# Retention in a two-layer diffusion trunk: tables first, rotation and zeta products on GpSimd, chunk states and chunk products as steps of the attention from the fifth pair of tiles on

## The chip, the cores and the metric

One core of a Trainium2 chip runs the whole program. The metric is the device time of one execution, in microseconds. The engines are TensorE (PE in the profile), VectorE (DVE), ScalarE (ACT), GpSimd (POOL) and SyncE (SP); each runs its own list of instructions strictly in order, and the lists meet through semaphores. DMA transfers are issued from the queues of SP (SPq) and ACT (ACTq).

## What is computed

The reference runs two layers on 128 context tokens and 1024 latent tokens (nine tiles of 128 rows; tile 8 is the context). In each layer one projection feeds four groups of heads (retention, Fourier mixing, latent attention, Hyena convolution), whose outputs go side by side through one output projection, and then a gated feed-forward layer follows. The change concerns the retention, which is run forward and backward over chunks of 128 rows:

```python
xi = jnp.exp((i[:, None] + 1.0) * log_gamma[None, :])
zeta = jnp.exp((C - 1.0 - i)[:, None] * log_gamma[None, :])
g_chunk = jnp.exp(C * log_gamma)
kv = jnp.einsum('bnchd,bnche->nbhde', kc * zeta[None, None, :, :, None], vc)

def step(S, kv_j):
    return g_chunk[None, :, None, None] * S + kv_j, S

s_final, s_prev = lax.scan(step, s0, kv)
cross = jnp.einsum('bnchd,nbhde->bnche', qc * xi[None, None, :, :, None], s_prev)
return (inner + cross).reshape(B, L, H, dv), s_final
```

Before that q and k of the latent rows are rotated (`axial_rope`); after it each head's output is normalised over its 64 channels and multiplied by a gate, `silu(rg) * o`.

## The kernel before, in words

A layer has three parts. `phase1` computes the projection and prepares the Hyena and latent-attention operands; `phase2` runs Fourier mixing, retention and attention; `phase3` multiplies the joined outputs by the output projection (tile name `wo`), and after it comes the feed-forward part.

**`phase2`.** The kernel is written in one order and a scheduler places each instruction on its engine's list, by the blocks' priorities (`tc.high_priority(offset=...)`) and by when its operands should be there; on the chip the lists are fixed. The Fourier part has offset 600. The retention's preparation has offset 100 and consists of three functions:

- `ret_rope` loads q and k of all tiles (`rqk`, 128x512 per tile) and rotates the eight latent tiles. The helper `rope` issues four products per tile, two of 128x256 into a scratch tile (`rtmp`) and two of 128x512 on `rqk`. They run on DVE.
- `ret_tables` makes the decay tables from eight numbers: `rzt` (zeta), `rgt` (chunk decay), `rxi` and the masks `rD` (some 25 DVE instructions on 128x8 and smaller, then four pairs of L1050 and L1051 on larger tiles). Its scratch lies in `Sall[:, 4:6]`.
- `ret_states` clears `Sall` (two memsets on POOL), then for each of the nine tiles forms k times zeta (`rkz`, two 128x256 products on DVE), multiplies it with v on PE (`pskv`, four groups), copies the blocks into `Sall` on ACT, and at the end runs the chain over the chunks in both directions on DVE (L161, 28 instructions).

**`attention`.** It runs over 20 pairs of tiles (four heads, per head four pairs of latent tiles and the context tile). At n it issues the scores of pair n (`sc` on PE, the scaled running minimum `pr` L930 on DVE, the exponential L933 on ACT), the transposes of pair n-1 (`pstr`, split into `ph`/`pl` or `pth`/`ptl` on ACT and DVE) and the product with v of pair n-2 (`po`); then it calls `beside(n)`, first at n = 2. In the kernel before `beside` takes one step of the retention's groups: `ret_group` handles three tiles (`ret_tile`, one step each), then a step of statistics (`rmu`, `rsq`, `rvr`, an inverse square root in eleven small DVE instructions) and a step of gating, in which `ro` (128x768) is multiplied on POOL and DVE, transposed on PE (`psr<-konst,ro`, L1173), copied to `rot` on ACT and stored to `mixR` from ACTq. Three groups of five steps fill n = 2 to 16.

**`phase3`.** SP loads the eight row blocks of the output projection (`woraw`, 512 KB each), which ACT and DVE split (`woh`, `wol`), and for each tile the four stored parts (`mix<-mixR`, `mixF`, `mixA`, `mixH`), split into `mixs`. Its memory is the memory that `phase2` gives back, so a load there waits until the last reader of what lay in its place is done.

Of the kernel before, what the change touches and what calls it, by code (L numbers as in the profile page):

```python
# [10 lines left out]
F32 = mybir.dt.float32  # L11
# [3 lines left out]
ALU = mybir.AluOpType  # L15
# [4 lines left out]
P = 128  # L20
# [3 lines left out]
CTX = 8  # L24
# [75 lines left out]
class Kern:  # L100
# [950 lines left out]
            V.tensor_tensor(out=Dm[:, h], in0=tm[:, 0], in1=tm[:, 1], op=ALU.add)  # L1051
        return zt, gt, Dm, xi

    def ret_rope(self, l, keep):

        nc = self.nc
        tabs = keep.tile([P, 2, 8, 64], F32, name="ropeR")
        nc.sync.dma_start(tabs, self.A["ropeR"])
        self.qk = keep.tile([P, NT, 512], F32, name="rqk")
        part = [keep.tile([P, 8, 64], F32, name="rtmp", tag=tg) for tg in ("rD", "rxi")]  # L1060
        for t in range(NT):
            if t % 3 == 0:
                nc.sync.dma_start(self.qk[:, t:t + 3], self.proj[l][:, t:t + 3, 256:768])
            if t < CTX:
                self.rope("v", self.qk[:, t].rearrange("p (h d) -> p h d", h=8), tabs[:, :, t], part[t % 2], 8, 64)
        return keep.tile([P, 8, 2, 2, P], F32, name="Sall")

    def ret_states(self, l, zt, gt, Sall, keep, pool, psp):


        nc, A = self.nc, self.A
        kvc = pool.tile([P, 4, P], F32, name="kvc", tag="rqkT")[:, 0:2].rearrange("p a (b e) -> p a b e", b=2)
        kzs = keep.tile([P, 2, 2, 4, 64], F32, name="rkz", tag="ropeR")
        for hh in range(2):
            nc.gpsimd.memset(Sall[64 * hh:64 * hh + 64, :, :, :, 64 - 64 * hh:P - 64 * hh], 0.0)
        for d in range(2):
            for hh in range(2):
                q = slice(64 * hh, 64 * hh + 64)
                nc.sync.dma_start(Sall[q, 7 * d, :, d, q], A["sret"][l, q, :, d])
        for t in range(NT):  # L1080
            if t % 3 == 0:
                v3 = pool.tile([P, 3, 512], F32, name="rv", tag="rvg")[:, :, 0:256]
                nc.sync.dma_start(v3, self.proj[l][:, t:t + 3, 768:1024])
            v = v3[:, t % 3]
            qk = self.qk[:, t].rearrange("p (h d) -> p h d", h=8)
            kz = kzs[:, t % 2]
            for d in range(2):
                self.tt("v", kz[:, d], qk[:, 4:8], zt[:, d].unsqueeze(2).broadcast_to([P, 4, 64]), ALU.mult)
            ps = psp.tile([P, 2, 2, P], F32, name="pskv", tag="r")
            for pr in range(2):  # L1090
                for d in range(2):
                    nc.tensor.matmul(ps[:, pr, d], kz[:, d, 2 * pr:2 * pr + 2].rearrange("p h d -> p (h d)"),
                                     v[:, P * pr:P * pr + P], start=True, stop=True)
            for hh in range(2):
                q = slice(64 * hh, 64 * hh + 64)
                if t == CTX:
                    nc.scalar.activation(kvc[q], ps[q, :, :, q], AF.Copy)
                    continue
                for d, dst in ((0, t + 1), (1, t - 1)):
                    if 0 <= dst < 8:  # L1100
                        nc.scalar.activation(Sall[q, dst, :, d, q], ps[q, :, d, q], AF.Copy)

        nc.sync.dma_start(A["o_st"][l], kvc)
        for d, order in ((0, range(1, 8)), (1, range(6, -1, -1))):
            for t in order:
                prev = t - 1 if d == 0 else t + 1
                for k in range(2):
                    self.stt(Sall[:, t, k, d], Sall[:, prev, k, d], gt[:, k, d:d + 1], Sall[:, t, k, d], ALU.mult, ALU.add)

    def ret_tile(self, l, t, vg, o, Dm, xi, Sall, pool, psp):  # L1110

        nc = self.nc
        lat = t < CTX
        nc.sync.dma_start(vg, self.proj[l][:, t, 768:1280])
        ps = psp.tile([P, 4, P], F32, name="psr", tag="r")
        for j in range(4):
            nc.tensor.transpose(ps[:, j], self.qk[:, t, j * P:j * P + P], self.ident)
        qkT = pool.tile([P, 4, P], F32, name="rqkT", tag="rqkT")
        nc.scalar.activation(qkT, ps, AF.Copy)
        if lat:  # L1120
            qx = pool.tile([P, 2, 2, P], F32, name="rqx")
            self.tt("g", qx, qkT[:, 0:2].unsqueeze(2).broadcast_to([P, 2, 2, P]), xi, ALU.mult)

        sT = pool.tile([P, 4, P], F32, name="rsT")
        pe = [psp.tile([P, 2, P], F32, name="psr", tag="r") for _ in range(2)]
        for e in range(2):
            q = slice(64 * e, 64 * e + 64)
            for pr in range(2):
                nc.tensor.matmul(pe[e][:, pr], qkT[q, 2 + pr], qkT[q, pr], start=True, stop=True)
            nc.vector.tensor_tensor(out=sT[:, e::2], in0=pe[e], in1=Dm[:, e::2], op=ALU.mult)  # L1130

        pi = psp.tile([P, 4, 64], F32, name="psr", tag="r")
        for pr in range(2):
            both = pi[:, 2 * pr:2 * pr + 2].rearrange("p h e -> p (h e)")
            if lat:
                nc.tensor.matmul(both, qx[:, pr, 0], Sall[:, t, pr, 0], start=True, stop=False)
            for h in (2 * pr, 2 * pr + 1):
                nc.tensor.matmul(pi[:, h], sT[:, h], vg[:, 64 * h:64 * h + 64], start=not lat, stop=not lat)
            if lat:
                nc.tensor.matmul(both, qx[:, pr, 1], Sall[:, t, pr, 1], start=False, stop=True)  # L1140
        nc.scalar.activation(o, pi, AF.Copy)
# [94 lines left out]
    def phase2(self, l):  # L1236
        nc, tc, A = self.nc, self.tc, self.A
        with ExitStack() as c:
            psp = Banks(c, tc, "ps2", {"tr": 2, "sc": 3, "po": 1, "r": 2})
            rp = c.enter_context(tc.tile_pool(name="rp", bufs=2, reuse_waits="tile"))  # L1240
            rk = c.enter_context(tc.tile_pool(name="rk", bufs=1, reuse_waits="tile"))
            with tc.tile_pool(name="fp", bufs=1, reuse_waits="tile", side="right") as fp, tc.high_priority(offset=600):
                self.fourier(l, fp, psp)
            with tc.high_priority(offset=100):
                Sall = self.ret_rope(l, rk)
                zt, gt, Dm, xi = self.ret_tables(l, rk, Sall)
                self.ret_states(l, zt, gt, Sall, rk, rp, psp)
            at = c.enter_context(tc.tile_pool(name="at", bufs=2, reuse_waits="tile", side="right"))
            hd = c.enter_context(tc.tile_pool(name="hd", bufs=1, reuse_waits="tile", side="right"))
            steps = (0 for g in range(3) for _ in self.ret_group(l, g, Dm, xi, Sall, rp, psp))  # L1250
            self.attention(l, at, hd, psp, lambda n: next(steps, None))
            for _ in steps:
                pass

# [473 lines left out]
```

## Time and profile before

| | us |
|---|---|
| median of three runs (lowest, highest) | 3415.93 (3404.67, 3424.79) |
| the profiled execution's own time | 3418.3 |
| its span in the profile | 3416.5 |

| engine | busy us | share of the span |
|---|---|---|
| PE | 3174.7 | 93% |
| DVE | 2118.5 | 62% |
| ACT | 1253.9 | 37% |
| POOL | 439.0 | 13% |

The share is an average over parts with different limits. The places that concern the change are the beginning of `phase2`'s attention (600 to 700 us in the first layer, 2280 to 2340 us in the second) and its end (820 to 860 and 2480 to 2520 us), and are read from stretches and from single instructions.

### The profile page before, as it was taken

The numbers are of one execution on the slowest core, as the hardware profiler recorded it, in microseconds if no ns is written. First come the engines' busy times: TensorE is split into PE (matmuls) and PEld (weight loads), VectorE is DVE, ScalarE is ACT, GpSimd is POOL, SyncE is SP. The second block draws the span as 40 slices with busy tenths as digits, with TensorE's granted clock in tenths as the row PEclk, the third lists the DMA queues.
The fourth block names the chain that finished last, engine by engine and source line by source line (L and its number), as shares of the span: only waits on it lengthen the run. The fifth ranks groups of instructions, "written<-read, shape, count | busy, mean of one in ns | idle before, by whom it ended". The sixth has DMA issues, their size and how long they took to land.

```text
span 3416.5 us, 52623 instructions
## 1 busy us (share of the span) xinstructions
PE 3174.7 (93%) x19870; PEld 2795.5 (82%) x19870; DVE 2118.5 (62%) x4362; ACT 1253.9 (37%) x2340; POOL 439.0 (13%) x420
## 2 busy tenths in 40 slices
PE   8889989799979999989999999889998999998998
PEld 5768767688879999988888788778887999998887
DVE  7552752777785555564667538648777866665554
ACT  3223212566652222233433232226667322223332
POOL 0110110010042222200000011101101422220000
PEclk9999999799989999999999899999998999999999
DMA  6443554313344444345654444432052322225564
GB/s 239 142 130 119 167 160 136 114 43 115 111 135 126 136 142 127 105 157 170 199 183 135 130 129 144 145 112 73 24 163 102 107 72 72 75 66 175 184 208 137
DMA packets 357023, 444.80 MB, mean 130 GB/s; under 512 B 70707, under 2 KB 287480, under 8 KB 356001
## 3 DMA queue, kind: packets, MB, share of 16 engines
q1 hardware_dynamic: 294992, 384.46, 36.2%
q10 hardware_dynamic: 61776, 56.97, 5.4%
q8 instruction: 157, 2.57, 0.3%
q14 instruction: 98, 0.79, 0.1%
HBM read 349.32 MB, written 92.00 MB: 129 GB/s over the span
## 4 chain that ended last, share of the span: by engine, by line
PE 63%; DVE 12%; DMA 6%; ACT 5%; issue 4%; POOL 2%; SPq 0%; DVEq 0%; ACTq 0%; POOLq 0%
PE gu L130 9%; PE gu L131 9%; PE gu L132 9%; PE dq L130 4%; PE dq L132 4%; PE dq L131 4%; PE acc L130 3%; PE acc L131 3%; PE acc L132 3%; PE psada L302 2%; DMA adw<-in_wada 1%; PE pstr L944 1%; DMA dwr<-in_wf 1%; PE po L961 1%; DVE x L158 1%
## 5 line engine op out<-in xcount | busy, mean ns | idle before, releaser
L130 PE MATMUL dq<-dw 128*128 128x512 f32 x792 | 310.1, 392 | 23.2 <-ACT dw L121 22.6
L131 PE MATMUL dq<-dw 128*128 128x512 f32 x792 | 309.9, 391 | 0.0
L132 PE MATMUL dq<-dw 128*128 128x512 f32 x792 | 309.2, 391 | 0.0
L130 PE MATMUL gu<-X,fw 128*128 128x256 f32 x1024 | 289.4, 285 | 1.0 <-DVE u L158 0.7
L132 PE MATMUL gu<-X,fw 128*128 128x256 f32 x1024 | 282.8, 279 | 3.4 <-DVE fw L126 3.4
L131 PE MATMUL gu<-X,fw 128*128 128x256 f32 x1024 | 282.7, 278 | 0.0
L130 PE MATMUL acc<-whi,Th 128*128 128x256 f32 (+1 forms) x720 | 215.7, 300 | 3.9 <-ACT whi L121 3.1
L131 PE MATMUL acc<-wlo,Th 128*128 128x256 f32 (+1 forms) x720 | 213.9, 297 | 2.3 <-DVE wlo L126 2.3
L132 PE MATMUL acc<-whi,Tl 128*128 128x256 f32 (+1 forms) x720 | 212.4, 295 | 0.0
L130 PEld LDWEIGHTS gu<-X,fw 128*128 128x128 f32 x1024 | 192.3, 189 | 20.4 <-issue 10.0
L126 DVE TENSOR_TENSOR dw<-dhr,dw 128x384 fp32r<-128x384 f32 x132 | 72.4, 554 | 205.8 <-ACT dw L121 205.7
L130 PEld LDWEIGHTS dq<-dw 128*128 128x128 f32 x792 | 149.6, 189 | 56.0 <-ACT dw L121 23.1
L132 PEld LDWEIGHTS gu<-X,fw 128*128 128x128 f32 x1024 | 192.5, 189 | 3.6 <-DVE fw L126 3.6
L131 PEld LDWEIGHTS gu<-X,fw 128*128 128x128 f32 x1024 | 192.5, 189 | 0.0
L130 PE MATMUL gu<-x1s,fw 128*128 128x320 f32 x576 | 178.7, 310 | 2.9 <-DVE u L158 2.5
L126 DVE TENSOR_TENSOR dw<-dwr,dw 128x1024 fp32r<-128x1024 f32 x132 | 161.1, 1221 | 31.7 <-ACT dw L121 31.6
L132 PE MATMUL gu<-x1s,fw 128*128 128x320 f32 x576 | 178.7, 310 | 1.8 <-DVE fw L126 1.8
L131 PE MATMUL gu<-x1s,fw 128*128 128x320 f32 x576 | 178.3, 310 | 0.0
L132 PEld LDWEIGHTS dq<-dw 128*128 128x128 f32 x792 | 149.5, 189 | 31.8 <-DVE dw L126 0.7
L131 PEld LDWEIGHTS dq<-dw 128*128 128x128 f32 x792 | 149.6, 189 | 30.5
L121 ACT ACTIVATE dw<-dhr 128x384 fp32r<-128x384 f32 x132 | 67.7, 516 | 251.6 <-PE dq L132 235.8
L121 ACT ACTIVATE dw<-dwr 128x1024 fp32r<-128x1024 f32 x132 | 138.3, 1049 | 53.1 <-DMA dwr<-in_wf 44.2
(496 smaller groups left out, 8910.0 us busy)
## 6 DMA issues: line engine op xcount, KB each, us to landing
dwr<-in_wf SPq DMA_DIRECT2D x132, 512.0 KB
adw<-in_wada SPq DMA_DIRECT2D x160, 256.0 KB
dhr<-h SPq DMA_DIRECT2D x132, 192.0 KB
h<-U SPq DMA_DIRECT2D x176, 128.0 KB
X<-in_wf SPq DMA_DIRECT2D x42, 512.0 KB
fr<-in_wf SPq DMA_DIRECT2D x40, 512.0 KB
pj<-pst ACTq DMA_DIRECT2D x90, 128.0 KB
G<-gt SPq DMA_DIRECT2D x36, 256.0 KB
```

The lines of the kernel that those rows point to most:

```text
L121: nc.scalar.activation(hi, src, AF.Copy)
L126: (nc.vector if elo == "dve" else nc.gpsimd).tensor_tensor(out=lo, in0=src, in1=hi, op=ALU.subtract)
L130: mm(ps, lh, rh, start=start, stop=False)
L131: mm(ps, lh, rl, start=False, stop=False)
L132: mm(ps, ll, rh, start=False, stop=stop)
L158: (self.nc.vector if e == "v" else self.nc.gpsimd).tensor_tensor(out=out, in0=a, in1=b, op=op)
L302: nc.tensor.matmul(ps[32 * j:32 * j + 32], self.konst[:, kt:kt + 249:8], ws[i + j // 2][:, j % 2], start=q == 0, stop=q > 0, tile_position ...
L944: T(pst[:, j], pr[i][:, (k0 + j) * P:(k0 + j + 1) * P], self.ident)
L961: nc.tensor.matmul(po[:, :nq], vhl[:, k], pth[:, i, :nq], start=i == 0, stop=False)
```

## The change

`ret_tables` is placed ahead of `ret_rope`, both at offset 600 (after the Fourier part). The rotation is issued to POOL and takes `Sall[:, 0:2]` as its scratch. The zeta products are issued to POOL. `ret_states` becomes a generator with three steps (after tiles 0 to 2, after tiles 3 to 5, after the rest with the chain over the chunks) and loses its offset. A new `retention` strings these three and the fifteen steps of the groups together, and `beside` takes a step only where n > 3, so that the eighteen steps fill n = 4 to 21.

```diff
-    def ret_rope(self, l, keep):
+    def ret_rope(self, l, keep, Sall):
...
-        part = [keep.tile([P, 8, 64], F32, name="rtmp", tag=tg) for tg in ("rD", "rxi")]
+        part = [Sall[:, i].rearrange("p a b (c d) -> p (a b c) d", d=64) for i in range(2)]
...
-                self.rope("v", self.qk[:, t].rearrange("p (h d) -> p h d", h=8), tabs[:, :, t], part[t % 2], 8, 64)
-        return keep.tile([P, 8, 2, 2, P], F32, name="Sall")
+                self.rope("g", self.qk[:, t].rearrange("p (h d) -> p h d", h=8), tabs[:, :, t], part[t % 2], 8, 64)
...
-                self.tt("v", kz[:, d], qk[:, 4:8], zt[:, d].unsqueeze(2).broadcast_to([P, 4, 64]), ALU.mult)
+                self.tt("g", kz[:, d], qk[:, 4:8], zt[:, d].unsqueeze(2).broadcast_to([P, 4, 64]), ALU.mult)
...
+            if t % 3 == 2 and t < CTX:
+                yield
...
+        yield
+
+    def retention(self, l, tabs, Sall, keep, pool, psp):
+
+        zt, gt, Dm, xi = tabs
+        yield from self.ret_states(l, zt, gt, Sall, keep, pool, psp)
+        for g in range(3):
+            yield from self.ret_group(l, g, Dm, xi, Sall, pool, psp)
...
-            with tc.high_priority(offset=100):
-                Sall = self.ret_rope(l, rk)
-                zt, gt, Dm, xi = self.ret_tables(l, rk, Sall)
-                self.ret_states(l, zt, gt, Sall, rk, rp, psp)
+            with tc.high_priority(offset=600):
+                Sall = rk.tile([P, 8, 2, 2, P], F32, name="Sall")
+                tabs = self.ret_tables(l, rk, Sall)
+                self.ret_rope(l, rk, Sall)
...
-            steps = (0 for g in range(3) for _ in self.ret_group(l, g, Dm, xi, Sall, rp, psp))
-            self.attention(l, at, hd, psp, lambda n: next(steps, None))
+            steps = self.retention(l, tabs, Sall, rk, rp, psp)
+            self.attention(l, at, hd, psp, lambda n: n > 3 and next(steps, None))
```

Lines after about L1110 stand nine further down in the changed kernel. What the change does to the lists is shown at three places. On PE, at the first layer's passage from Fourier mixing (`psx`) to the scores (`sc`), the list of before has

```order
L1207 MATMUL psx<-fcons,fin 128x256
L1214 MATMUL psx<-fx,fch 128x128
L1215 MATMUL psx<-fx,fch 128x128
L1226 MATMUL psx<-ffc,fin 128x256
L1230 MATMUL psx<-fx,fch 128x128
L1231 MATMUL psx<-fx,fch 128x128
L1226 MATMUL psx<-ffc,fin 128x256
L1230 MATMUL psx<-fx,fch 128x128
L1231 MATMUL psx<-fx,fch 128x128
L130 MATMUL sc<-at_Tl_5479,at_Th_5478 128x384
```

and the changed one

```order
L1216 MATMUL psx<-fcons,fin 128x256
L1091 MATMUL pskv<-rv,rkz 128x128
L1223 MATMUL psx<-fx,fch 128x128
L1224 MATMUL psx<-fx,fch 128x128
L1235 MATMUL psx<-ffc,fin 128x256
L1091 MATMUL pskv<-rv,rkz 128x128
L1239 MATMUL psx<-fx,fch 128x128
L1240 MATMUL psx<-fx,fch 128x128
L1091 MATMUL pskv<-rv,rkz 128x128 x2
L1235 MATMUL psx<-ffc,fin 128x256
L1091 MATMUL pskv<-rv,rkz 128x128 x3
L1239 MATMUL psx<-fx,fch 128x128
L1240 MATMUL psx<-fx,fch 128x128
L1091 MATMUL pskv<-rv,rkz 128x128 x13
L130 MATMUL sc<-at_Tl_5341,at_Th_5340 128x384
```

Twenty `pskv` matmuls (five tiles) have moved ahead of the scores; only the first nine score matmuls (three groups), which stand earlier in both lists, are still in front of them. On POOL, the first layer's list from the rotation's end on reads in the changed kernel (`Sall` in the first row is the rotation's scratch)

```order
L158 TENSOR_TENSOR rqk<-rqk,Sall 128x512
L158 TENSOR_TENSOR rkz<-rqk,rzt 128x256
L1074 MEMSET Sall 64x32x64 x2
L158 TENSOR_TENSOR rkz<-rqk,rzt 128x256 x17
L158 TENSOR_TENSOR rqx<-rqkT,rxi 128x512 x3
```

All 32 instructions of the rotation stand ahead of the first zeta product (in the second layer too, where eight zeta products stand ahead of the memsets). Before, POOL had only the memsets and the `rqx` products here. At the end of the attention, in both layers, PE's list of before has the retention's last transposes among the scores of the last pairs, about a hundred rows ahead of the first `wo`:

```order
L962 MATMUL po<-ptl,vhl 128x256
L1173 MATMUL psr<-konst,ro 128x128 x4
L961 MATMUL po<-pth,vhl 128x256
L130 MATMUL sc<-at_Tl_6849,at_Th_6848 128x384
L1173 MATMUL psr<-konst,ro 128x128 x2
L131 MATMUL sc<-at_Tl_6849,at_Th_6848 128x384
```

In the changed one they stand behind the last `po` and directly ahead of `wo`:

```order
L964 MATMUL po<-konst,mx 128x128 x2
L961 MATMUL po<-pth,vhl 128x128
L962 MATMUL po<-ptl,vhl 128x128
L964 MATMUL po<-konst,mx 128x128
L1182 MATMUL psr<-konst,ro 128x128 x6
L130 MATMUL wo<-woh_7849,mixs 128x512
L131 MATMUL wo<-wol_7850,mixs 128x512
```

On SP the eight loads `woraw` stood together ahead of the first `mix`; now two stand there, seven loads of `phase3` and the feed-forward part follow, and then the other six, directly ahead of the first `mix`:

```order
L1277 DMA woraw<-in_wout 128x1024 x2
...
L1298 DMA c_8752<-mod_4_252 128x8x1
L1277 DMA woraw<-in_wout 128x1024 x6
L1288 DMA mix<-mixR_0_98 128x256
L1289 DMA mix<-mixF_152 128x2x128
```

## Rows read from the trace of the kernel before

**Rows 1.** Windows of the first layer: length, busy us per engine, PEclk, DMA share, GB/s.

```profile
600.00:640.00 40.00, 28.55 (x101) 21.00 (x101) 30.30 (x102) 13.11 (x33) 0.00 (x0) 0.62 0.45 142
640.00:700.00 60.00, 52.91 (x383) 47.74 (x382) 48.20 (x145) 37.04 (x91) 8.96 (x6) 0.94 0.21 61
820.00:840.00 20.00, 15.59 (x110) 14.54 (x109) 17.88 (x35) 14.99 (x25) 0.00 (x0) 0.91 0.47 154
840.00:860.00 20.00, 20.00 (x92) 16.62 (x91) 11.91 (x18) 6.09 (x9) 4.32 (x3) 1.00 0.71 196
```

**Rows 2.** Window in the second layer, in which its first states are formed.

```profile
2320.00:2340.00 20.00, 17.30 (x126) 16.09 (x126) 18.74 (x59) 13.22 (x46) 5.01 (x3) 0.91 0.45 121
```

**Rows 3.** Timeline, first layer: start, us, engine, instruction [idle before <-releaser].

```profile
604.52 1.07 DVE L158 TENSOR_TENSOR rtmp<-rqk,ropeR 128x256 f32<-128x256 f32 x3
629.02 0.55 DVE L930 TENSOR_SCALAR_CACHE_REDUCE pr<-sc 128x384 f32<-128x384 f32 x1
629.63 0.69 PE L130 MATMUL sc<-at_Tl,at_Th 96*128 96x384 f32 x1 [1.45 <-DVE pr L930]
```

**Rows 4.** Timeline of PE, second layer, around the rotation and first states.

```profile
2305.12 1.08 PE L944 MATMUL pstr<-konst,pr 128*128 128x128 f32 x4 [14.70 <-DVE rt L1017]
2321.10 3.81 PE L1092 MATMUL pskv<-rv,rkz 128*128 128x128 f32 x18
```

**Rows 5.** Groups of DVE by form, 600 to 660 us: busy us, mean ns.

```profile
L158 DVE TENSOR_TENSOR rkz<-rqk,rzt 128x256 f32<-128x256 f32 x18 | 7.0, 421 | 0.2
L158 DVE TENSOR_TENSOR rqk<-rqk,ropeR 128x512 f32<-128x512 f32 x8 | 5.5, 682 | 0.0
```

**Rows 6.** Groups of POOL by form, whole span.

```profile
L158 POOL TENSOR_TENSOR rqx<-rqkT,rxi 128x512 f32<-128x512 f32 x16 | 20.6, 1286 | 155.2 <-ACT rqkT L1119 155.2
L158 POOL TENSOR_TENSOR ro<-ro,rmu 128x768 f32<-128x768 f32 x6 | 8.8, 1472 | 48.0 <-DVE rmu L1153 48.0
L1075 POOL MEMSET Sall<- 64x2048 f32 x4 | 7.2, 1798 | 178.4 <-DVE rD L1051 178.3
L158 POOL TENSOR_TENSOR hy_t<-hy_a 128x256 f32<-128x256 f32 x8 | 6.8, 846 | 0.0
```

**Rows 7.** Timelines of POOL and DVE where both work on SBUF.

```profile
577.27 4.70 POOL L158 TENSOR_TENSOR fab<-fin 128x1024 f32<-128x1024 f32 x2 [109.61 <-DMA fch<-in_chan]
...
579.70 2.81 DVE L158 TENSOR_TENSOR fab<-fab 128x512 f32<-128x512 f32 x1 [8.37 <-POOL fab L158]
...
117.75 8.47 POOL L158 TENSOR_TENSOR mlau<-mlau,krt 128x256 f32<-128x256 f32 x1
```

**Rows 8.** Groups of DVE and ACT by form, 780 to 840 us.

```profile
L1152 DVE TENSOR_REDUCE rmu<-ro 128x12 f32<-128x768 f32 x1 | 1.0, 951 | 0.0
L1169 DVE SCALAR_TENSOR_TENSOR ro<-rth,ro 128x768 f32<-128x768 f32 x1 | 1.0, 958 | 0.6 <-POOL ro L158 0.6
L150 DVE TENSOR_TENSOR rq_w<-rq_w,rvr 128x12 f32<-128x12 f32 x3 | 0.5, 157 | 0.0
...
L126 DVE TENSOR_TENSOR mixs<-mix,mixs 128x1024 fp32r<-128x1024 f32 x2 | 2.4, 1218 | 0.8 <-ACT mixs L121 0.8
...
L1156 ACT ACTIVATE rsq<-ro 128x768 f32<-128x768 f32 x1 | 0.8, 833 | 0.0
```

**Rows 9.** Timelines at the end of the first layer's attention (PE, ACT, SP).

```profile
812.03 0.66 PE L1173 MATMUL psr<-konst,ro 128*128 128x128 f32 x4 [0.21 <-DVE ro L1169]
...
815.42 0.33 ACTq L1176 DMA_DIRECT2D mixR<-rot  x1
...
822.65 1.00 SPq L1279 DMA_DIRECT2D mix<-mixR  x1
...
832.31 0.32 SPq L1279 DMA_DIRECT2D mix<-mixR  x1
...
836.71 1.06 ACT L121 ACTIVATE mixs<-mix 128x1024 fp32r<-128x1024 f32 x1 [1.87 <-DMA mixA<-o]
...
837.78 0.48 PE L130 MATMUL wo<-woh,mixs 128*128 128x512 f32 x1
```

## The prediction

> **What bounds the kernel now.** PE is the bound over the whole, so I asked the windows where it stands idle beside the code that changes. In the first layer it is idle 40 - 28.6 = 11.4 us from 600 to 640 and 7.1 us from 640 to 700, with DVE busy 30 and 48 us there [rows 1]: the attention starts behind DVE. The timeline says with what: DVE turns the tiles from 604.52 on, and only at 629.02 makes the first scaled scores (`pr`); PE, whose first nine score matmuls had long filled the three banks, goes on at 629.63 [rows 3]. In the second layer the same rotation holds PE for 14.70 us at one place, up to 2305.12, and the first `pskv` run at 2321.10 [rows 4]; DVE stays nearly full after that, 18.7 of 20 us, with PE idle 2.7 us [rows 2]. At the other end of the attention there is no gap: retention's last transposes are at 812.03 and the first `wo` matmul stands right behind the last `po` at 837.78 [rows 9], in a stretch with 4.4 us of idle PE; the 20 us after it have none [rows 1]. So time lost before `wo` is not won back soon after.
>
> **The rotation on POOL.** 32 instructions of a layer leave DVE: eight tiles times two of 128x256 and two of 128x512. What they cost on POOL is read from its own rows: a 128x512 product 1.286 us (`rqx`, run amid the attention); a 128x256 one between half of that, 0.64, and 0.846 (`hy_t`) [rows 6]. I take 0.80, as `hy_t` has the right size. 8 x (2 x 0.80 + 2 x 1.286) = 33.4 us; the ends are 30.9 and 34.1. On DVE one of 128x512 is 0.68 [rows 5]: whoever waits for the rotation waits twice as long.
>
> The zeta products cost POOL 18 x 0.80 = 14.4 us a layer and free DVE of 18 x 0.421 = 7.6 us [rows 5]; the memsets keep their 2 x 1.80 [rows 6].
>
> **First layer, start.** q and k are loaded a few rows later on SP than before, behind four small tables; I let POOL start where DVE did, 604.5. POOL then needs 33.4 us (637.9), one zeta product (638.7), the memsets (642.3) and nine more zeta products (649.5), and the twenty `pskv` that its list has ahead of the scores need ten zeta products. DVE's list has six chain instructions (L161) ahead of the first `pr`, which need the third tile's `pskv`, that is POOL until about 646, with PE, ACT and DVE behind it. So the scores go on at about 650 and not at 629.6: 20 us later. Of this comes back: PE's idle 7.1 us of 640 to 700 [rows 1], since DVE has 7.6 us of zeta products and most of the tables behind it, and about 2.5 us of `pskv` already done (18 take 3.81 us at mixed clocks [rows 4]; 20 at the rate of their later part). That is 9.5. Loss: **+11 us**, between +3 (POOL at its lower price, all of DVE's relief used) and +21 (nothing comes back).
>
> **Second layer, start.** The 14.70 us stall goes, as DVE goes on with `pr` while POOL turns the tiles. But PE's list has its first `pskv` behind the same 63 score matmuls as before, and POOL, if it starts where the stall began (2305.12 - 14.70 = 2290.4), has the four zeta products for them only at 2290.4 + 33.4 + 4 x 0.80 = 2327, against 2321.10: PE runs ahead and then waits. 6 us late, of which the relieved DVE gives back the 2.7 us of idle PE [rows 2]: **+3 us**, between -8 (DVE's relief goes on working) and +9.
>
> **The port.** A DVE instruction on two SBUF operands that met POOL's `fab` pair (4.70 us for two) took 2.81 us, not 0.68; and POOL's 128x256 product at 117.75, amid DVE's work, took 8.47 us, not 0.8 [rows 7]. POOL's rotation meets some 20 such DVE instructions of the tables, most of 0.16 us [rows 8]. If each delays POOL by 0.16 to 0.42 us (the length of a `rkz` [rows 5]) that is 3 to 8 us a layer; I take 4 for each: **+8 us** in all, from 0 (they find gaps) to 24.
>
> The Trainium skill (SBUF — State Buffer, "two separate sides") calls the port pair of VectorE and GpSimd an exclusive lock, held for a whole instruction, also for a VectorE instruction with two SBUF inputs against a GpSimd one that reads SBUF; the rows on `fab` agree. By that rule nearly every meeting waits, and the sum takes the upper end, 24 us instead of 8: 3490.
>
> **End of the attention, both layers.** Eighteen steps on n = 4 to 21 put the last tile at n = 19, the statistics at 20 and the gate at 21, where no pair is left but the context's. Behind the last tile's products PE has some sixteen `po` matmuls, about 3 us at the 0.21 us of a `pskv` [rows 4]. The chain to the gate is two reductions (0.95 each), two POOL products (1.47 each), a square (0.83), eleven small instructions (0.16, about 0.2 with their gaps) and the last product (0.96) [rows 6, 8], with the copy to `ro` about 9.5 us: PE waits 6.5 us for its last six transposes. Then `wo` needs the stored `mixR` and the split weights. On SP six of the eight `woraw` now stand behind the retention's memory, the third needs `ro` read, the last the store of `mixR_8`; only then the first `mix` is loaded. Before, the store's issue came 3.4 us after the transposes, the first `mix` load 7.2 us after that, and from a `mix` load to its split 4.4 us, then the two splits 1.06 and 1.22 [rows 8, 9]. Together 17.3 us; on idle engines I take 15.5, of which 1 is PE's transposes. 6.5 + 14.5 = 21 us; the retention's last steps now fill the 4.4 us that PE is idle in the last pairs [rows 1], which gives back 3. **+18 us a layer, +36**; the ends are +12 (the store lands at once) and +25 a layer. PE also stands still so long that it restarts slowly: the granted clock was 0.62 in the gaps of 600 to 640 and 0.91 in those of 820 to 840 [rows 1]; that is in the upper end.
>
> **The sum.** 11 + 3 + 8 + 36 = +58 us on the profiled execution's 3418.3 us: 3476. That execution was 2.4 us above the median of the runs shown: **3474 us**. All lower ends together give 3 - 8 + 0 + 24 = +19, all upper ones 21 + 9 + 24 + 50 = +104; the terms are of separate places and will hardly all fall to one side.
>
> **Rivals.** *The relief wins (faster).* DVE loses 15 + 7.6 us a layer. If POOL is never waited for, PE's idle 18.5 us of 600 to 700 and the 14.7 + 2.7 us of the second layer come back, 36 us, and with the end at its lower price of 2 x 12 = 24 the kernel gains 12: 3404, or 3380 if the end too is hidden. It decides at POOL's rotation: it would have to be done 20 us earlier, half of its price. For it speaks how full DVE is there; against it the order, in which the scores stand behind `pskv`. Chance 0.12. *The ends meet (no change).* POOL is waited for, but DVE's relief over the rest of the attention pays for that and for 10 us more, and the end costs its lower price, 24: 3416 to 3433. Chance 0.12. *The end alone.* The start is neutral and the end costs 36 to 44: 3452 to 3460; the relief is then worth what POOL's wait costs. It is near the forecast; 0.2. *The port decides.* Each rotation is stretched by another 8 us, and the chain (28 of L161 on two SBUF operands beside POOL's zeta products) too: +20, 3495. Chance 0.12. The forecast itself has 0.44.
>
> **The numbers.** A measurement of this kernel can tell about 0.5%, 17 us, from no change: 3399 to 3433. Faster 0.12, same 0.12, slower 0.76. The range leaves out the faster case and the top of the port's: 3414 to 3510.
>
> **What would show it.** In the changed profile: POOL busy some 48 us a layer more; the rotation from about 605 to 638 on POOL; PE idle up to about 650 in the first layer with `pskv` waiting on POOL's `rkz`; no 14.7 us stall on DVE in the second, but one on `rkz` near 2325; PE idle some 20 us between the last `po` and the first `wo`, in two pieces, before `psr<-konst,ro` (on DVE `ro`) and before `wo` (on `mixs`). I am wrong if PE passes from `po` to `wo` in under 8 us, or if the first `pr` of the first layer comes before 635.

## The result, and the profile after

The changed kernel takes 3459.16 us (median of four runs, 3454.01 to 3461.62) against 3415.63 us: a ratio of 1.0125, 95% interval 1.0098 to 1.0153, or +43.5 us. The forecast was 3474 us, slower. The profiled execution has a span of 3456.2 us, 39.7 more than before.

The windows of the first layer, in the same stretches as [rows 1], and of the second layer as in [rows 2]:

```profile
600.00:640.00 40.00, 15.96 (x50) 10.27 (x50) 21.16 (x50) 9.56 (x29) 30.58 (x32) 0.59 0.38 128
640.00:700.00 60.00, 55.84 (x375) 51.00 (x376) 45.94 (x142) 38.34 (x91) 17.06 (x22) 0.90 0.30 86
820.00:840.00 20.00, 15.88 (x133) 14.28 (x131) 11.44 (x29) 9.25 (x22) 2.74 (x2) 0.99 0.31 90
840.00:860.00 20.00, 1.80 (x6) 1.01 (x6) 11.50 (x21) 8.40 (x12) 5.67 (x4) 0.50 0.81 274
2320.00:2340.00 20.00, 3.19 (x15) 2.00 (x15) 11.98 (x21) 5.65 (x15) 19.92 (x21) 0.61 0.17 44
```

PE lost 12.6 us of busy time from 600 to 640 (16.0 for 28.6) while POOL worked for 30.6 of the 40 us, and nearly everything from 840 to 860, where `wo` had run without a gap: 1.8 us for 20.0. At the first place PE has two long waits, and in the second layer one more, which the timeline of PE shows (the bracket is the idle time before and what ended it):

```profile
622.93 1.19 PE L1218 MATMUL psx<-fcons,fin 128*128 128x256 f32 x2 [9.43 <-DVE fab L1230]
...
641.54 0.80 PE L1091 MATMUL pskv<-rv,rkz 128*128 128x128 f32 x2 [8.73 <-POOL rkz L158]
...
2340.02 3.93 PE L1091 MATMUL pskv<-rv,rkz 128*128 128x128 f32 x16 [12.41 <-POOL rkz L158]
```

The last is the second layer's, where the 14.70 us behind DVE [rows 4] are gone and 12.41 us behind POOL's zeta products have come. At the end of the attention the timeline of PE has, in the first layer and (the second pair) in the second,

```profile
845.48 1.85 PE L1182 MATMUL psr<-konst,ro 128*128 128x128 f32 x6 [6.90 <-DVE ro L1178]
...
864.21 0.79 PE L130 MATMUL wo<-woh,mixs 128*128 128x512 f32 x1 [16.88 <-ACT mixs L121]
...
2520.18 1.85 PE L1182 MATMUL psr<-konst,ro 128*128 128x128 f32 x6 [6.89 <-DVE ro L1178]
...
2537.87 0.79 PE L130 MATMUL wo<-woh,mixs 128*128 128x512 f32 x1 [15.85 <-ACT mixs L121]
```

where [rows 9] had `wo` right behind `po` (twelve `wo` matmuls even run ahead of the last four of `po` there, without a gap): 6.9 us for the gate, 1.85 for the six transposes, 16 to 17 for what `wo` needs. What that is, SP's and ACT's timelines say:

```profile
846.20 0.38 ACT L1184 ACTIVATE rot<-psr 128x256 f32<-128x256 f32 x1 [3.12 <-PE psr L1182]
...
847.36 8.42 SPq L1277 DMA_DIRECT2D woraw<-in_wout  x6
855.83 0.42 SPq L1288 DMA_DIRECT2D mix<-mixR  x1
...
849.88 0.38 ACT L1184 ACTIVATE rot<-psr 128x256 f32<-128x256 f32 x1 [2.51 <-DMA mixR<-rot]
...
861.22 1.06 ACT L121 ACTIVATE woh<-woraw 128x1024 fp32r<-128x1024 f32 x1 [0.28 <-DMA woraw<-in_wout]
863.10 2.05 ACT L121 ACTIVATE mixs<-mix 128x1024 fp32r<-128x1024 f32 x2 [0.83 <-DMA mix<-mixH]
```

The six weight loads are issued from 847.36 on, the last just ahead of the first `mix` at 855.83; ACT splits the last of them at 861.22. What they wait for on SP is the retention (SP's waits, 838 to 866 us: total, times, longest):

```profile
SPq L1277 <- DMA mixR<-rot: 6.0, 3, 2.2
SPq L1277 <- PE psr L1182: 1.9, 1, 1.9
SPq L1277 <- DVE ro L1178: 0.9, 1, 0.9
```

Even the third `rot` waits: its buffer is one of two and has to be stored first (2.51 us).

On POOL the groups by form, 600 to 700 us, answer to [rows 6]:

```profile
L158 POOL TENSOR_TENSOR Sall<-rqk,ropeR 128x256 f32<-128x256 f32 x16 | 11.9, 754 | 23.1 <-ACT fq L1226 23.1
L158 POOL TENSOR_TENSOR rkz<-rqk,rzt 128x256 f32<-128x256 f32 x18 | 11.4, 650 | 9.6 <-PE pskv L1091 9.2
L158 POOL TENSOR_TENSOR rqk<-rqk,Sall 128x512 f32<-128x512 f32 x8 | 10.4, 1297 | 0.1
L158 POOL TENSOR_TENSOR rqk<-rqk,ropeR 128x512 f32<-128x512 f32 x8 | 10.3, 1284 | 0.0
```

The rotation came to 11.9 + 10.4 + 10.3 = 32.6 us of busy time, forecast 33.4; the zeta products to 0.65 us each, forecast 0.80.

### The profile page after: what moved, and what is told of

Same layout as the page of the kernel before. It is cut to its first block, busy times and chain, and to the rows that moved or that the text cites. A ratio compares the mean times of both kernels' runs of the same rounds, so it can differ in the third digit from the quotient of the medians.

```text
span 3456.2 us, 52642 instructions
## 1 busy us (share of the span) xinstructions
PE 3170.5 (92%) x19870; PEld 2797.4 (81%) x19870; DVE 2101.7 (61%) x4262; ACT 1256.6 (36%) x2340; POOL 520.2 (15%) x520
## 4 chain that ended last, share of the span: by engine, by line
PE 65%; DVE 10%; DMA 6%; ACT 4%; issue 3%; POOL 3%; SPq 0%; DVEq 0%; ACTq 0%; POOLq 0%
PE gu L130 9%; PE gu L131 9%; PE gu L132 9%; PE dq L130 4%; PE dq L132 4%; PE dq L131 4%; PE acc L130 3%; PE acc L131 3%; PE acc L132 3%; PE psada L302 2%; PE pstr L944 1%; POOL rqk L158 1%; PE wo L130 1%; PE wo L132 1%; PE po L961 1%
## 5 line engine op out<-in xcount | busy, mean ns | idle before, releaser
L130 PE MATMUL dq<-dw 128*128 128x512 f32 x792 | 310.3, 392 | 23.7 <-ACT dw L121 23.2
L130 PEld LDWEIGHTS gu<-X,fw 128*128 128x128 f32 x1024 | 192.6, 189 | 19.6 <-issue 8.7
```

What stands on the lines that cost most here:

```text
L130: mm(ps, lh, rh, start=start, stop=False)
```

## The experiments

The theory: the loss is made at the attention's end, because the retention finishes behind it, and the late start is mostly given back. The main rival: the loss is made at the start, by GpSimd's rotation. A second rival: the order of SP's loads or the states as steps cost by themselves.

All of them at a glance. "First layer" is how much later than before the profile shows the first matmul `gu` of the feed-forward part (951.1 us before); "second layer" how much longer the stretch from the first Fourier matmul `psx` to the first `gu` is (407.0 us before); "gaps" are PE's time from the last `po` to the first `wo` in the two layers. The measured ratio and median stand beside them, each against the runs of the kernel before on the same chip (medians 3415.6 to 3418.8).

| kernel | first layer | second layer | gaps | median us | ratio, 95% interval |
|---|---|---|---|---|---|
| the change | +26.3 | +18.3 | 25.6, 24.6 | 3459.16 | 1.0125 [1.0098, 1.0153] |
| e1: before, late steps | +22.3 | +17.3 | 24.7, 24.4 | 3450.04 | 1.0099 [1.0069, 1.0130] |
| e2: GpSimd start alone | +5.1 | +8.7 | none | 3431.54 | 1.0043 [1.0025, 1.0061] |
| e3: change, n = 2 to 16 | +5.0 | +3.3 | none | 3427.90 | 1.0031 [1.0011, 1.0050] |
| e4: change, rotation on DVE | +18.3 | +14.0 | 27.9, 23.2 | 3444.52 | 1.0086 [1.0063, 1.0109] |
| e5: e3, rotation on DVE | +1.1 | -4.3 | none | 3407.76 | 0.9978 [0.9960, 0.9995] |
| e6: e3, rotation after tables | +19.6 | +5.4 | none | 3439.47 | 1.0067 [1.0046, 1.0088] |
| e7: e3, rotation shared | -5.5 | -1.9 | none | 3416.17 | 1.0002 [0.9985, 1.0020] |
| e8: change, n = 2 to 19 | +18.4 | +18.8 | 12.4, 14.3 | 3457.70 | 1.0116 [1.0089, 1.0142] |
| e9: e5, zeta on DVE | -5.3 | -2.8 | none | 3411.37 | 0.9972 [0.9954, 0.9989] |
| e10: n = 4 to 15, rotation on DVE | -4.6 | +0.4 | below 1 | 3408.15 | 0.9975 [0.9962, 0.9989] |
| e11: n = 4 to 15 | +9.0 | +2.3 | below 1 | 3424.66 | 1.0018 [1.0003, 1.0033] |

The two stretches together give the measured difference to within 8 us in every line (the change: 44.6 for 43.5), so the larger differences are made in them. The first column counts from the start of the execution; of it 0.3 to 7.0 us (4.2 in the change, 7.0 in e1) had passed before the first layer's first `psx`, ahead of the code that the edits concern.

A second measure is PE's idle time from the first `psx` to the first `gu`, where all kernels have the same matmuls. In the two layers it is 37 and 44 us before, 64 and 62 in the change, 53 and 63 in e1, 51 and 48 in e3, 54 and 60 in e4, 37 and 45 in e5, 36 and 45 in e10, 50 and 46 in e11. By it the late end costs 14 to 19 us in either layer (e1 against before, the change against e11), and the rotation on GpSimd 11 to 14 us in the first layer and only 1 to 3 in the second (the change against e4, e3 against e5, e11 against e10).

### e1: the end alone

```diff
-            self.attention(l, at, hd, psp, lambda n: next(steps, None))
+            self.attention(l, at, hd, psp, lambda n: n > 6 and next(steps, None))
```

(an edit of the kernel before)

> The kernel before with its fifteen retention steps moved from n = 2 to 16 to n = 7 to 21, and nothing else; the rotation, the zeta products and the states stay as they were. Theory (the loss is made at the attention's end, by the retention finishing behind it): the loss of the change comes back whole, some 23 to 27 us a layer in two waits of PE, on `ro` and on `mixs`: +45 to +55 us, 3460 to 3470. Rival (the loss is made at the attention's start, by GpSimd): within 10 us of the kernel before, 3406 to 3426.

Measured: 3450.04 us, ratio 1.0099, +33 us. Not the whole 45 to 55, but most of the change's 43.5, and far from the rival's. PE's waits from 838 to 880 us and from 2500 to 2550 us (total, times, longest) are those of the change to a microsecond:

```profile
PE wo L130 <- ACT mixs L121: 15.9, 1, 15.9
PE psr L1173 <- DVE ro L1169: 6.9, 1, 6.9
...
PE wo L130 <- ACT mixs L121: 15.7, 1, 15.7
PE psr L1173 <- DVE ro L1169: 6.9, 1, 6.9
```

With nothing of the retention's preparation changed, gaps of 24.7 and 24.4 us cost 33 us and not 49: the attention itself ends sooner, in the first layer its last `po` 246 us after the first `psx` for 258 before. That fits the forecast that the retention's last steps fill idle time of PE in the last pairs, and they partly lie behind it.

### e2: the start alone

```diff
-            steps = self.retention(l, tabs, Sall, rk, rp, psp)
-            self.attention(l, at, hd, psp, lambda n: n > 3 and next(steps, None))
+            with tc.high_priority(offset=100):
+                for _ in self.ret_states(l, *tabs[:2], Sall, rk, rp, psp):
+                    pass
...
+            zt, gt, Dm, xi = tabs
+            steps = (0 for g in range(3) for _ in self.ret_group(l, g, Dm, xi, Sall, rp, psp))
+            self.attention(l, at, hd, psp, lambda n: next(steps, None))
```

> The changed kernel with the states formed ahead of the attention at offset 100 and the groups' steps at n = 2 to 16 again, so that only tables first, rotation and zeta products on GpSimd are left of the change. Theory: the start is neutral to slightly better, -12 to +6 us, 3404 to 3422, with the first scaled scores some 25 us late in the first layer and nearly all of it given back by the attention's end. Rival: the first layer's late start stays, +15 to +25 us, 3430 to 3440.

Measured: 3431.54 us, ratio 1.0043, +15 us: the lower end of the rival's range. My "neutral start" falls. With e1's 33 it makes 48, near the change's 43.5, so the two causes are separate and nearly additive, and the states as steps may give a little back.

### e3 and e11: the change with an earlier end

```diff
-lambda n: n > 3 and next(steps, None)
+lambda n: [next(steps, None) for _ in range(2 if n < 5 else 1)]
```

> The changed kernel with all its parts, but the eighteen steps taken at n = 2 to 16 (two each at n = 2, 3 and 4), so that the last gate stands at n = 16 as before. Theory: PE passes from `po` to `wo` without a gap and the change becomes neutral to slightly better, -12 to +6 us, 3404 to 3422. Rival (SP's loads or the states as steps cost by themselves): 3430 to 3460.

Measured: 3427.90 us, 1.0031. PE has no gap at `wo`; the change keeps +11 us, above the 6 that the theory allowed and just under the rival's range. e11 leaves the beginning at n = 4 as the change has it:

```diff
-lambda n: n > 3 and next(steps, None)
+lambda n: n > 3 and [next(steps, None) for _ in range(2 if n < 10 else 1)]
```

> The change as it stands with one edit: two steps at a time from n = 4 to 9, one from 10 to 15, so that the last gate stands at n = 15; the rotation stays on GpSimd. Theory: the loss at the end goes and the rotation's loss stays, as in the third experiment: 3420 to 3432. If beginning at the fifth pair hides GpSimd's rotation, 3405 to 3415.

Measured: 3424.66 us, 1.0018 [1.0003, 1.0033]. One line, which says when the steps are taken, takes back 37 of 43.5 us (1.0125 - 1.0018 = 1.07%). PE still waits for POOL there, in the first layer (600 to 860 us) and the second (2240 to 2520 us):

```profile
PE pskv L1091 <- POOL rkz L158: 10.4, 3, 9.4
PE psx L1218 <- DVE fab L1230: 10.2, 1, 10.2
...
PE pskv L1091 <- POOL rkz L158: 12.4, 1, 12.4
```

### e4, e5 and e10: the rotation back on VectorE

The edit, in `ret_rope` of the change (e4), of e3 (e5) and of e11 (e10):

```diff
-                self.rope("g", self.qk[:, t].rearrange("p (h d) -> p h d", h=8), tabs[:, :, t], part[t % 2], 8, 64)
+                self.rope("v", self.qk[:, t].rearrange("p (h d) -> p h d", h=8), tabs[:, :, t], part[t % 2], 8, 64)
```

> The changed kernel with the rotation back on VectorE, all else as changed (late steps, zeta products on GpSimd). Theory: the loss at the end stays and the start changes little: 3450 to 3470. Rival (the rotation on GpSimd costs the time): most of the loss goes, 3415 to 3435.

Measured: 3444.52 us, 1.0086: the gaps at the end stay (27.9 and 23.2 us), and the rotation on DVE is worth 0.39% (13 us). It lies under the theory's 3450, because the start does matter.

> The changed kernel with the rotation on VectorE and the steps at n = 2 to 16 (both edits of the second and third experiment's kind together): left of the change are tables first, the zeta products on GpSimd and the states as steps. Theory (late end some +33 to +40 us, rotation on GpSimd some +15 us, the rest a gain): -4 to -12 us against the kernel before, 3405 to 3413. Rival (the rest of the change is worth nothing or the two losses share a cause): 3414 to 3430.

Measured: 3407.76 us, 0.9978 [0.9960, 0.9995]: -8 us, as expected, and 0.53% (18 us) under e3.

> The change as it stands with two edits: the rotation on VectorE, and two steps at a time from n = 4 to 9, one from 10 to 15, so that the steps still begin at the fifth pair and the last gate stands at n = 15. Theory: no waits before `wo`, and the states are wanted two pairs later than in the fifth experiment: 3400 to 3410. If the start at n = 4 is worth nothing, it equals the fifth experiment, 3408.

Measured: 3408.15 us, 0.9975 [0.9962, 0.9989], the same as e5, so no difference is seen between steps that begin at n = 2 and at n = 4. Against e11 it shows the rotation's price a third time, 0.43% (15 us). In the second layer the stall behind DVE is back in all three, 17.1 to 17.2 us (e10, 2240 to 2520 us):

```profile
PE pstr L911 <- DVE pl L126: 17.1, 1, 17.1
```

That is longer than the 12 to 13 us for which PE waits there when POOL turns the tiles, and PE's idle time in that layer is nearly the same either way: as idle time, the price of POOL's rotation lies in the first layer. By the table's columns it is 4 to 14 us in the first layer and 2 to 8 in the second.

### e9: the zeta products back on VectorE

```diff
-                self.tt("g", kz[:, d], qk[:, 4:8], zt[:, d].unsqueeze(2).broadcast_to([P, 4, 64]), ALU.mult)
+                self.tt("v", kz[:, d], qk[:, 4:8], zt[:, d].unsqueeze(2).broadcast_to([P, 4, 64]), ALU.mult)
```

(an edit of e5)

> The fifth experiment's kernel with the zeta products back on VectorE too, so that only tables first and the states as steps (n = 2 to 16) are left of the change. If the fifth experiment's gain of 8 us comes from the states as steps and the tables, this stays at 3404 to 3412; if it comes from the zeta products on GpSimd (7.6 us of VectorE time a layer), the gain goes: 3412 to 3422.

Measured: 3411.37 us, 0.9972 [0.9954, 0.9989]: the gain stays, so the zeta products on GpSimd are worth nothing that can be seen (the two ratios can be told apart to some 8 us); the gain of 7 to 10 us comes from tables first and the states as steps. These two were not told apart.

### e6: the port

```diff
-        part = [Sall[:, i].rearrange("p a b (c d) -> p (a b c) d", d=64) for i in range(2)]
+        part = [Sall[:, 4 + i].rearrange("p a b (c d) -> p (a b c) d", d=64) for i in range(2)]
```

(an edit of e3: the rotation's scratch now overlaps the tables' scratch, so POOL begins when DVE has done the tables)

> The changed kernel with the steps at n = 2 to 16 and with the rotation's scratch laid where the tables' scratch lies (Sall[:, 4:6]), so that GpSimd's rotation can begin only when VectorE has finished the tables and the two no longer meet. Theory of the shared port: the tables' small VectorE instructions, which took 0.6 to 1.2 us each beside the rotation, take 0.17 again and PE's wait of 9.4 us in the Fourier part goes; the rotation starts some 8 to 12 us later, so that the time stays within 8 us of the third experiment's 3428. Rival (the small instructions are slow for another reason): they stay at 0.6 to 1.2 us.

In the change the tables' small instructions on DVE (128x8) were held as soon as POOL's rotation began, at 609.35; DVE's timeline before and after that moment:

```profile
608.20 0.17 DVE L1022 TENSOR_SCALAR rt<-rt 128x8 f32<-128x8 f32 x1
...
610.13 0.64 DVE L1021 TENSOR_TENSOR rt<-rt,rt 128x8 f32<-128x8 f32 x1
610.80 0.65 DVE L1022 TENSOR_SCALAR rt<-rt 128x8 f32<-128x8 f32 x1
611.49 1.18 DVE L1021 TENSOR_TENSOR rt<-rt,rt 128x8 f32<-128x8 f32 x1
```

In e6 the same instructions at the same place, and POOL's first rotation, are

```profile
611.10 0.17 DVE L1022 TENSOR_SCALAR rt<-rt 128x8 f32<-128x8 f32 x1
611.30 0.17 DVE L1021 TENSOR_TENSOR rt<-rt,rt 128x8 f32<-128x8 f32 x1
...
622.58 2.19 POOL L158 TENSOR_TENSOR Sall<-rqk,ropeR 128x256 f32<-128x256 f32 x3 [37.52 <-DVE Sall L1050]
```

so the meeting of the two engines is what made them slow, and PE's 9.43 us wait in the Fourier part is gone. But the kernel gains nothing by it: POOL's rotation starts 13.2 us later than in the change (622.58 for 609.35), PE waits 19.0 and 20.6 us at one place for `rkz` in the two layers, and the time rises to 3439.47 us, 12 us above e3 where I allowed 8 (PE's waits, 600 to 860 and 2240 to 2545 us).

```profile
PE pskv L1091 <- POOL rkz L158: 19.0, 1, 19.0
...
PE pskv L1091 <- POOL rkz L158: 20.8, 2, 20.6
```

It is the end of POOL's work that PE waits for at the start.

### e7: the rotation shared

```diff
-                self.rope("g", self.qk[:, t].rearrange("p (h d) -> p h d", h=8), tabs[:, :, t], part[t % 2], 8, 64)
+                self.rope("gv"[t % 2], self.qk[:, t].rearrange("p (h d) -> p h d", h=8), tabs[:, :, t], part[t % 2], 8, 64)
```

(an edit of e3)

> The changed kernel with the steps at n = 2 to 16 and the rotation dealt out by turns, even tiles on GpSimd and odd ones on VectorE. If the two engines work side by side, the rotation takes some 16 us (four tiles at 4.0) and the time is at or under the kernel before: 3405 to 3415. If each instruction holds the other engine off, the rotation takes 24 to 26 us (4 x 4.0 + 4 x 2.2), each VectorE product is seen near 1.3 to 2 us, and the time is between the third experiment and the kernel before: 3416 to 3428.

Measured: 3416.17 us, 1.0002 [0.9985, 1.0020], on the boundary of the two ranges, so the time does not decide. The timelines do, in part: POOL's four tiles ran from 606.05 to 625.3, 19.3 us for a forecast 16 alone, and DVE's last rotation product ended at 630.3, 24 us after the first. A DVE product of 0.41 and one of 0.68 took up to 1.11 and 1.64 us beside them:

```profile
617.39 1.53 POOL L158 TENSOR_TENSOR rqk<-rqk,ropeR 128x512 f32<-128x512 f32 x1
619.00 1.59 POOL L158 TENSOR_TENSOR rqk<-rqk,Sall 128x512 f32<-128x512 f32 x1
...
617.83 1.64 DVE L158 TENSOR_TENSOR rqk<-rqk,ropeR 128x512 f32<-128x512 f32 x1
...
623.10 1.11 DVE L158 TENSOR_TENSOR Sall<-rqk,ropeR 128x256 f32<-128x256 f32 x1
```

Sharing the work saves 8 of the 32 us of the rotation on POOL alone, not half: each engine lengthens the other's instructions.

### e8: two pairs earlier

```diff
-lambda n: n > 3 and next(steps, None)
+lambda n: next(steps, None)
```

> The changed kernel with the steps from the first call on, at n = 2 to 19, so that the last gate stands two pairs earlier than in the change. How steep the loss at the end is: if the chain behind the last gate must simply fit under the attention's remaining 7 us of PE work, PE's two waits before `wo` shrink from 24.5 to some 10 to 15 us a layer, 3440 to 3452; if SP's loads of the weights stay behind the retention whatever the distance, they stay above 18 us, 3453 to 3462.

Measured: 3457.70 us, 1.0116 [1.0089, 1.0142], which is the second of the two ranges by the time, and not told apart from the change. By the profile the first was right about the gaps: PE waits for the gate 0.7 us at most, and the wait for `mixs` is 12.4 and 14.3 us. (PE's waits, 600 to 860 us.)

```profile
PE wo L130 <- ACT mixs L121: 12.4, 1, 12.4
PE pskv L1091 <- POOL rkz L158: 12.3, 3, 11.3
```

The gaps are 13 and 10 us shorter than in the change, but the time is not: e8 lies 30 us above e3, whose steps also begin at n = 2, and its two gaps make 26.7 us. Outside the gap PE is idle 49 and 47 us from the first `psx` to the first `gu`, as in e3 (51 and 48), where the change has 40 and 40. So e8 pays its gaps in full, and what comes back in the change does not come back here. The likeliest reading is that the retention's last steps moved back in front of the last `po` and no longer fill PE's idle time there; no run separates this.

## Why the prediction was right, point by point

- **The sign and the main term were right.** "End of the attention, +36 us" is confirmed by four differences: e1 against before +33 us, the change against e3 0.94% (32 us), against e11 1.07% (37 us), e4 against e5 1.08% (37 us). Inside the term the parts stand as forecast: the gate wait 6.9 us for 6.5, then 1.85 + 16.9 = 18.7 and 1.85 + 15.85 = 17.7 us for 15.5. What comes back is more than the forecast 3 us a layer: gaps of 49 us cost e1 only 33, so about 8 a layer. So the fit of the sum is in part luck: the gaps came to 25 us a layer for 21, and the 4 too little there are made up by the 5 too little that come back.
- **The start was oversized.** The terms "first layer +11", "second layer +3" and "the port +8" make 22 us. e2 measures +15 for tables first, rotation and zeta products on POOL together; with the states as steps and no late end, e3 has +11 and e11 +6. That is about the 15 us by which 3474 is above 3459. Three steps of it:
  - "20 us later" for the first scaled scores was right: 654.42 for 629.02, 25.4 us, or 21 counted from the first `psx`. "Of this 9.5 comes back" is the step that failed. In e3 the first `pr` comes at 652.2, 23 us late, and the feed-forward part begins 5.0 us late: about 18 came back. One part of the error is a count: the twenty `pskv` of PE's list are 40 records in the trace (72 for the layer's 36), and before the first 40 took PE 5.3 us in the first layer, not 2.5. For the whole, PE is idle 14 us longer in e3 than before from the first `psx` to the first `gu`, but busy 11 us less for the same 1972 records (320 for 331), at a granted clock of 0.94 for 0.92. Its busy time is shorter in e5, e9 and e10 too (322 to 328), where POOL turns no tile. So a good part of what came back belongs to tables first and the states as steps, which the forecast had in the sum only as DVE's relief, and not to the late start; how it divides between the clock and closer packing stays open.
  - The second layer's +3 was right in size: e3 has +3.3, with the 14.70 us stall replaced by one of 12 to 13 us on `rkz`, as the text foresaw.
  - "The port, +8 us" was right as a mechanism and wrong in its direction. POOL was hardly delayed: its rotation took 31.6 us from its beginning to its end (609.35 to 640.92) and 31.1 in e6, where it does not meet the tables. DVE was, 0.6 to 1.2 us for 0.17, and PE behind it by 9.43 us; but that delay lies under the longer wait for POOL, and e6, which removes it and starts POOL 13.2 us later, has a first layer 14.6 us longer than e3's. So no cost of it is seen; with POOL's start left as it was, it was not tried. The upper end of 24 us, and with it the 3490, has no working in the rows, which give 6 to 16, and it did not come.
- **The rival that came nearest** is "the end alone" (3452 to 3460, chance 0.2), by its number. Its mechanism, a neutral start, holds only as a sum: about +15 for the rotation (13, 15 and 18 us in three comparisons) and -7 to -10 for tables first and the states as steps.
- **"The relief wins" fell.** Freeing DVE of the zeta products gave nothing (e5 against e9), and the rotation's relief on DVE cost more on POOL than it gave.
- **The marks** that I named were all seen but one number: POOL has 520.2 us of busy time for 439.0, 40.6 us a layer and not 48, since a 128x256 product cost 0.65 to 0.75 and not 0.80, and neighbours on POOL overlap by some 0.03 us.

The experiments give versions that beat both kernels, if by little: e9 (tables first and the states as steps, steps ended at n = 16, rotation and zeta products on VectorE) at 0.9972, e10 at 0.9975, e5 at 0.9978; the three can't be told apart.

## What to carry to other kernels

Work that fills gaps beside a main loop has to end early enough for everything behind it: here a chain of 10 us to the gate, a store, and weight loads whose memory it still held, some 24 us a layer in which PE stood still, of which 16 to 18 remained as loss, for moving the last step by five pairs. Before moving such steps, follow the last one to its consumers, through the DMA queue and through the memory that is given back. And work given to an engine half as fast is only free if nobody waits for its result: PE's list asked for it at a fixed place. A wait that the profile shows is not yet its price, either: in the second layer a stall of 17 us behind DVE and a wait of 13 us for POOL left PE idle about equally long.

## What the runs showed of the hardware that was not expected

- A DVE instruction with one SBUF operand on 128x8, TENSOR_SCALAR, was held beside POOL's rotation like those with two: 0.65 us for 0.17 (the rows under e6). The Trainium skill (SBUF — State Buffer, "two separate sides") names instructions with two SBUF inputs and those in a 2-port mode, which it says `tensor_scalar` can enter; whether this one was in it, the runs don't show.
- DVE got through about once per POOL instruction: with POOL busy without a pause, DVE's small instructions took about the length of one POOL product each (0.64 and 1.18 us beside products of 0.72 and 1.26), and POOL's own took at most 0.90 and 1.47. The 8.47 us of [rows 7] are there again at that place in the changed kernel (8.47 us at 120.03), but nothing like it is in the rotation.
- Between 1900 and 1940 us, in a part that the change does not touch, the granted clock was 0.74 in the profile of the kernel before and 1.00 in that of the change. e3, e5 and e7 had 0.74, 0.70 and 0.74, and e1 0.88 there and 0.78 in the 40 us after; e4, e6, e8, e9 and e11 had 1.00, e2 and e10 0.96 and 0.97. The stretch from the first layer's `wo` to the second's `psx` was 9 us longer in the profile of before (1379.1 for 1370.2 us); it took 1379 to 1385 us in the five profiles with the lower clock and 1369 to 1376 in the others. Whether this makes the spread of single executions of one kernel was not measured, and what decides the clock stayed open.
